# Two pairs of the MLP's first product in step, factors formed on VectorE, and x loaded by ScalarE

## The chip, the cores and the metric

One core of a Trainium2 chip runs the whole kernel. The metric is device time in microseconds, of the one core that is used.

## What is computed

One block of a transformer in float32, for x of 1024 tokens by 1024 features: a norm, a projection to queries, keys, values and gates, two kinds of attention (one with compressed, selected and windowed keys, one with a sliding window and a sink), and then what matters here:

```
y = sigmoid(gate_a) * (o_a @ w_up_nsa) + sigmoid(gate_b) * (o_b @ w_up_swa)
h = x + rms_norm(y @ w_out, norm_mix_post)
u = rms_norm(h, norm_mlp_pre)
f = square(relu(u @ w_mlp_in)) @ w_mlp_out        # 1024 -> 4096 -> 1024
out = h + rms_norm(f, norm_mlp_post)
```

## The kernel before, in words

The kernel is written in a tile language: the program states operations on named tiles and pools of buffers, and a scheduler puts them into one queue for each engine. It keeps to the order of the program as a priority, estimates times, and issues what is ready by that estimate, so the order on an engine can differ from that of the text. A pool has a number of buffers for each tag; a new tile of the tag waits until the tile that had its buffer has been read for the last time. Pools that are opened later lie on the memory of pools that were closed, and wait for their tiles in the same way.

**Float32 by three matmuls.** TensorE (PE) reads a reduced format. Each operand is therefore split into a high part (a copy by ScalarE into that format) and a low part (the difference of source and high part): `split`, L84 to L91. A product is high x high, high x low and low x high (`mm3`, L122 to L125; `prod`, L927 to L932). `load_w` (L95 to L116) loads a weight into a raw buffer, makes the high part on ScalarE (L107) and the low part in two pieces: columns of the first `cut` eighths on VectorE, the rest on GpSimd (L115, here 640 and 384 of 1024 columns). With `l_eng` given, one engine makes the whole low part (L105).

**Output projection.** `out_proj` (L806 to L830) is called four times, for two blocks of 128 tokens each; each call loads w_out again in eight pieces of 512 KB, issued by SP, with two raw buffers. The blocks of x that are added later (`load_x`, L834) are loaded by SP too: blocks 0, 1, 4 and 5 ahead of the first projection call, the others as buffers come free. `norm_a` adds x and writes h to memory, `norm_b` makes u, and `norm_t` (L855) transposes a block of u and forms factors of it.

**MLP, first product.** u @ w_mlp_in uses Winograd's form of Strassen's product: seven half-size products instead of eight, with factors that are sums of the quarters. The token half 0 gives the quarters 1 and 2 (bh0, bl0), made in `norm_t` of blocks 0 to 3, which also keep a float32 copy (braw). From `norm_t` of blocks 4 to 7, with its two transposed halves pts[0] and pts[1], come the factors 5, 3, 6, 4 and 7 for the right side:

```
t1 = pts[0] - braw_lo        # factor 5, low part by VectorE
b22 = pts[1]                 # factor 3, low part by GpSimd
t2 = b22 - t1                # factor 6, low part by VectorE
t4 = t2 - braw_hi            # factor 4, formed by GpSimd, low part by GpSimd
t3 = b22 - pts[0]            # factor 7, low part by GpSimd
```

All of this is done for the blocks 4 to 7 in `norm_t` (L870 to L877), with a small pool of four buffers. Products 1 and 2 need only the token half 0: `head` (L936 to L949) does them for a pair of column blocks of w_mlp_in. The heads of the first four pairs are issued ahead, beside the norms and transposes of blocks 5 to 7 (L953 to L961). `mlp1` (L973 to L1033) then goes through 16 pairs, one after the other: it loads two raw weights, has GpSimd form four sums of them (L992 to L995), splits five left operands (L998 to L1000), and does products 5, 3, 6, 4 and 7 of 12 matmuls each, with sums of their results (p5, c12, c21, c22) and, by GpSimd, four further sums q. Results go to memory for the second product. From pair 4 on, `mlp1` does its own head first: 84 matmuls a pair.

**What sets the order.** SP issues nearly all transfers, in one queue; where an issue waits for its buffer, those behind it wait too. VectorE, ScalarE and GpSimd run their queues in order. PSUM has six banks for results (tag ps) and two for transposes (tag pt); the four heads ahead hold four of the six.

Of the kernel before, what the change touches and what calls it, by code (L numbers as in the profile page):

```python
# [15 lines left out]
P = 128  # L16
# [36 lines left out]
def tile_hybrid_block(ctx: ExitStack, tc: tile.TileContext, x, norm_mix_pre, norm_mix_post, norm_mlp_pre,  # L53
# [39 lines left out]
    nw = [0]  # L93

    def load_w(parts, shape, wpool=None, hb=2, l_eng=None, rpool=None, rb=2, cut=5, tag="w"):  # L95
# [10 lines left out]
        else:  # L106
            nc.scalar.activation(h, raw, AF.Copy)  # L107
# [631 lines left out]
    with ExitStack() as s:  # L739
# [45 lines left out]
        wp2 = s_w2.enter_context(pool("wq"))  # L785
        s_e = s.enter_context(ExitStack())
# [10 lines left out]
        braw = ep.tile([P, NB, 512], F32, name="braw")  # L797
# [8 lines left out]
        def out_proj(c, ts_, nhs):  # L806
            pss = {(t, nh): ps_any() for t in ts_ for nh in nhs}
            n = 1024 // (512 * len(nhs))
            for k2 in range(NB // n):
                wh, wl = load_w([(None, wor[:, n * k2:n * k2 + n, 512 * nhs[0]:512 * nhs[-1] + 512])],  # L810
                                [n, 512 * len(nhs)], *((wp2, 2) if not started else (we, WEB)), cut=CUT[c], rpool=wp2)
# [22 lines left out]
        def load_x(b):  # L834
            hbs[b] = hb_e[b] if b in hb_e else (we if b < 4 else ea).tile([P, D], F32, name="hb", tag="hb", bufs=2)
            nc.sync.dma_start(hbs[b], x[b * P:(b + 1) * P, :])
# [18 lines left out]
        def norm_t(b):  # L855
# [4 lines left out]
            for k0 in range(0, NB, 4):  # L860
# [3 lines left out]
                if b < 4:  # L864
                    split(bh0[:, k0:k0 + 4, bs], bl0[:, k0:k0 + 4, bs], pt)
                    nc.scalar.activation(braw[:, k0:k0 + 4, bs], pt, AF.Copy)
# [3 lines left out]
            b22, t1, t3, t2, t4 = (e2.tile([P, 4, P], F32, name="bt", tag="bt", bufs=4) for _ in range(5))  # L870
            nc.scalar.activation(b22, pts[1], AF.Copy)
            nc.vector.tensor_tensor(t1, pts[0], braw[:, 0:4, bs], op=ALU.subtract)
            nc.vector.tensor_tensor(t3, b22, pts[0], op=ALU.subtract)
            nc.vector.tensor_tensor(t2, b22, t1, op=ALU.subtract)
            nc.gpsimd.tensor_tensor(t4, t2, braw[:, 4:8, bs], op=ALU.subtract)
            for i, (op_, src) in enumerate(((5, t1), (3, b22), (6, t2), (4, t4), (7, t3))):
                split(bh[op_][:, :, bs], bl[op_][:, :, bs], src, l_eng="pool" if i in (1, 3, 4) else "dve")  # L877

        load_x(0)
        load_x(1)  # L880
        load_x(4)
        load_x(5)
        out_proj(0, (0, 1), (0, 1))
# [6 lines left out]
        out_proj(0, (2, 3), (0, 1))  # L890
# [12 lines left out]
        e2 = s_e.enter_context(pool("e2"))  # L903
# [3 lines left out]
        for i in (5, 3, 6, 4, 7):  # L907
            bh[i] = u1.tile([P, 4, 512], F32R, name=f"bh{i}")
            bl[i] = u1.tile([P, 4, 512], F32R, name=f"bl{i}")
        bh[1], bl[1], bh[2], bl[2] = bh0[:, 0:4], bl0[:, 0:4], bh0[:, 4:8], bl0[:, 4:8]  # L910
# [42 lines left out]
        for p in range(NPRE):  # L953
            head(p, fp0, load_wcols(w_mlp_in, 2 * p * P, P, wp2, rpool=wp2))
# [4 lines left out]
            if p == 1:  # L959
                norm_t(6)  # L960
                norm_t(7)  # L961
        s_e.close()
# [4 lines left out]
        fp = s_m1.enter_context(pool("f"))  # L967
# [5 lines left out]
        def mlp1(p):  # L973
# [8 lines left out]
            if p in pre:  # L982
                xb, c11, _ = pre[p]
                s1 = fp.tile([P, 512], F32, name="p5", tag="p5", bufs=2)
# [50 lines left out]
        for p in range(NPAIR):  # L1035
            mlp1(p)
# [191 lines left out]
```

## Time and profile before

| what | value |
|---|---|
| median of three runs | 1590.59 us (1589.45 to 1592.19) |
| the profiled execution | 1591.69 us |
| its span, first to last instruction | 1589.9 us |
| mean granted clock of TensorE | 0.98 |
| PE busy (matmuls) | 1483.0 us, 93% of the span |
| VectorE (DVE) busy | 1068.0 us, 67% |
| ScalarE (ACT) busy | 749.0 us, 47% |
| GpSimd (POOL) busy | 488.8 us, 31% |
| memory traffic | 133 GB/s over the span |

The profile is that of one execution; its sums are held against its own time. Times inside it count from the start of the span. The output projection runs from about 794 to 918 us, the heads and transposes to 954, the pairs of `mlp1` to 1271, and then comes the second product. Where a line of the profile ends in a bracket, it gives the idle time of the engine before the instruction and what ended it. PE is TensorE, PEld its weight loads, SPq the queue of SyncE.

### The profile page before, as it was taken

What the parts mean: (1) busy time and instruction counts of PE and PEld (TensorE: products, weight loads), DVE (VectorE), ACT (ScalarE), POOL (GpSimd) and SP (SyncE); (2) the same over time, 40 slices, a digit from 0 to 9 for tenths busy, and PEclk for the clock granted to TensorE, in tenths of its full rate; (3) what the DMA queues carried; (4) which work ended last, traced back from release to release, by engine and by line L of the source; (5) the groups of instructions that cost most, each with busy time, mean ns of one, the idle gap of its engine ahead of it and who ended that gap; (6) DMA issues with size and microseconds to landing.
All of it is one profiled execution on the core that took longest, in us unless ns stands there. A gap on an engine that the chain in (4) does not pass through costs nothing. (4 is left out here: it accounts for less than half of the span.)

```text
span 1589.9 us, 20194 instructions
## 1 busy us (share of the span) xinstructions
PE 1483.0 (93%) x6920; PEld 1210.6 (76%) x6920; DVE 1068.0 (67%) x2070; ACT 749.0 (47%) x1453; POOL 488.8 (31%) x390
## 2 busy tenths in 40 slices
PE   6998999999999999999978885999999999999997
PEld 5897888778777787788756664787888778888886
DVE  5554774698865988836527686576766467495775
ACT  5343774566644776554236553332332324334443
POOL 3000351122311322331035457566666410000302
PEclk9999999999999999999989997999999999999999
DMA  7733124111132111164256652445443588353451
GB/s 210 248 98 81 37 57 146 45 39 34 31 97 61 37 34 38 34 235 151 69 206 213 210 156 67 140 156 164 155 147 128 205 314 323 98 185 112 153 186 53
DMA packets 162039, 204.80 MB, mean 129 GB/s; under 512 B 15120, under 2 KB 105264, under 8 KB 161936
## 3 DMA queue, kind: packets, MB, share of 16 engines
q1 hardware_dynamic: 154800, 182.78, 36.5%
q0 software_dynamic: 6992, 20.48, 3.6%
q8 instruction: 54, 0.88, 0.2%
q14 instruction: 49, 0.40, 0.1%
q10 hardware_dynamic: 144, 0.26, 0.0%
HBM read 153.02 MB, written 58.32 MB: 133 GB/s over the span
## 5 line engine op out<-in xcount | busy, mean ns | idle before, releaser
L123 PE MATMUL mm<-uh,wh 128*128 128x512 f32 x464 | 200.9, 433 | 4.6 <-DVE qb L447 3.2
L509 POOL TENSOR_TENSOR e<-e,w 128x256 f32<-128x256 f32 (+7 forms) x128 | 111.8, 900 | 284.2 <-DVE w L647 148.2
L124 PE MATMUL mm<-ul,wh 128*128 128x512 f32 x464 | 184.3, 397 | 0.0
L125 PE MATMUL mm<-uh,wl 128*128 128x512 f32 x464 | 184.2, 397 | 0.0
L87 ACT ACTIVATE th<-pt 128x512 fp32r<-128x512 f32 (+1 forms) x178 | 105.3, 593 | 94.7 <-PE pt L519 84.3
L501 ACT ACTIVATE e<-e,nm 128x256 f32<-128x256 f32 (+7 forms) x192 | 124.4, 649 | 36.1 <-DVE nm L495 35.5
L91 DVE TENSOR_TENSOR tl<-pt,th 128x512 fp32r<-128x512 f32 x162 | 110.1, 683 | 33.3 <-ACT th L87 32.1
L115 POOL TENSOR_TENSOR wl<-wraw,wh 128x384 fp32r<-128x384 f32 (+2 forms) x46 | 70.7, 1540 | 200.1 <-ACT wh L107 196.1
L87 ACT ACTIVATE fh<-fraw 128x1024 fp32r<-128x1024 f32 x56 | 59.6, 1063 | 148.0 <-PE xs L1121 70.2
L930 PE MATMUL ps<-bh,ws_h 128*128 128x512 f32 x256 | 102.9, 404 | 21.0 <-ACT ws_h L87 16.2
L91 DVE TENSOR_TENSOR fl<-fraw,fh 128x1024 fp32r<-128x1024 f32 x56 | 69.6, 1243 | 75.6 <-ACT fh L87 74.9
L519 PE MATMUL pt<-ident,e 128*128 128x128 f32 x648 | 104.4, 275 | 1.9 <-DVE e L512 0.9
L1144 POOL TENSOR_TENSOR cc<-cc,gB 128x512 f32<-128x512 f32 x14 | 24.3, 1762 | 262.4 <-ACT sq L1143 260.6
L125 PEld LDWEIGHTS mm<-uh,wl 128*128 128x128 f32 x464 | 87.6, 189 | 20.7
L1121 PE MATMUL xs<-vl,fh 128*128 128x512 f32 x256 | 99.7, 390 | 3.6 <-DVE vl L91 3.6
L931 PE MATMUL ps<-bl,ws_h 128*128 128x512 f32 x256 | 102.6, 401 | 0.0
L123 PEld LDWEIGHTS mm<-uh,wh 128*128 128x128 f32 x464 | 88.5, 191 | 18.1 <-issue 3.3
L932 PE MATMUL ps<-bh,ws_l 128*128 128x512 f32 x256 | 101.7, 401 | 0.2 <-DVE ws_l L91 0.2
L1121 PE MATMUL xs<-vh,fl 128*128 128x512 f32 x256 | 99.6, 389 | 0.0
L1121 PE MATMUL xs<-vh,fh 128*128 128x512 f32 x256 | 99.4, 389 | 0.0
L519 PEld LDWEIGHTS pt<-ident,e 128*128 128x128 f32 x648 | 81.4, 141 | 22.7 <-issue 2.3
L124 PEld LDWEIGHTS mm<-ul,wh 128*128 128x128 f32 x464 | 88.7, 191 | 12.0
(273 smaller groups left out, 3947.8 us busy)
## 6 DMA issues: line engine op xcount, KB each, us to landing
fraw<-f_d SPq DMA_DIRECT2D x48, 512.0 KB, 3.6
wraw<-in_w_mlp_in_dram SPq DMA_DIRECT2D x36, 512.0 KB, 4.2
wraw<-in_w_out_dram SPq DMA_DIRECT2D x32, 512.0 KB, 3.6
f_d<-q SPq DMA_DIRECT2D x64, 256.0 KB, 2.3
b<-in_w_mlp_out_dram SPq DMA_DIRECT2D x32, 512.0 KB, 10.8
wraw<-in_w_in_dram SPq DMA_DIRECT2D x27, 512.0 KB, 4.6
f_d<-c SPq DMA_DIRECT2D x48, 256.0 KB, 2.3
gate_d<-gst SPq DMA_DIRECT2D x32, 256.0 KB, 2.1
```

What stands on the lines that cost most here:

```text
L87: nc.scalar.activation(h, src, AF.Copy)
L91: eng.tensor_tensor(l, src, h.bitcast(F32), op=ALU.subtract)
L123: nc.tensor.matmul(ps, ah, bh, start=first, stop=False)
L124: nc.tensor.matmul(ps, ah, bl, start=False, stop=False)
L125: nc.tensor.matmul(ps, al, bh, start=False, stop=last)
L501: nc.scalar.activation(e[:, :n], e[:, :n], AF.Exp, scale=-1.0, bias=nm[:, r:r + 1], accum_out=sm[:, r:r + 1])
L509: nc.gpsimd.tensor_tensor(res[r][:, :n], res[r][:, :n], w[:, r:r + 1].to_broadcast([P, n]), op=ALU.mult)
L519: tr = nc.tensor.transpose(pt[:rows, r, :], es[r][:, off:off + rows], ident)
L930: nc.tensor.matmul(ps, ah[:, k, :], bh[i][:, k, :], start=n[0], stop=False, skip_group_check=True)
L931: nc.tensor.matmul(ps, ah[:, k, :], bl[i][:, k, :], start=False, stop=False, skip_group_check=True)
L932: nc.tensor.matmul(ps, al[:, k, :], bh[i][:, k, :], start=False, stop=n[1], skip_group_check=True)
L1121: nc.tensor.matmul(bank[t], l_[:, j, ts], r_[:, j, :], start=a_, stop=z_, skip_group_check=True)
```

## The change

- The factors 3, 6, 4 and 7 are no longer formed in `norm_t`. It forms factor 5 only and keeps both transposed halves in float32 (b12, b22, in the buffers that factor 7 takes later). A new function `factor(i, b)` forms one factor of one block, wholly by VectorE with the high part by ScalarE.
- The first two pairs of `mlp1` run in step, product by product: 5, 5, 3, 3, 6, 6, 4, 4, 7, 7. Factor 3 is formed ahead of them, factor 6 after the two products 5, factor 4 after the products 3, factor 7 after the products 6. `mlp1` becomes a generator; it splits each left operand just ahead of its product instead of all five together. From pair 2 on the pairs go one after the other as before.
- The low parts of the weights of the projection's second half (`c` = 1, eight loads in each of two calls) and of the four heads are made by VectorE alone.
- The x blocks 0 and 1 are issued by ScalarE behind the high part of weight 4 in the first projection call, the blocks 4 and 5 behind weight 3 in the second.
- Buffers: a new pool cq of eight 2 KB buffers holds the raw quarters (braw), and after them the results c and q; the pools of left operands and of p5 are cut differently; x blocks 0 to 3 have a pool of their own, which also holds t1.

```diff
+    last_act = [None]
@@ load_w
-            nc.scalar.activation(h, raw, AF.Copy)
+            last_act[0] = nc.scalar.activation(h, raw, AF.Copy)
@@
+        cq = s_w2.enter_context(pool("cq"))
+        braw = {(b, h): cq.tile([P, 4, P], F32, name="braw", tag="cq", bufs=8) for b in range(4) for h in range(2)}
@@
-        braw = ep.tile([P, NB, 512], F32, name="braw")
+        eh = s_e.enter_context(pool("etmph"))
+        hb_e.update({b: eh.tile([P, D], F32, name="hb", tag="hb", bufs=2) for b in (0, 1)})
@@
-        def out_proj(c, ts_, nhs):
+        def out_proj(c, ts_, nhs, xs_=(), at=0):
...
-                                [n, 512 * len(nhs)], *((wp2, 2) if not started else (we, WEB)), cut=CUT[c], rpool=wp2)
+                                [n, 512 * len(nhs)], *((wp2, 2) if not started else (we, WEB)), cut=CUT[c], rpool=wp2, l_eng="dve" if c else None)
+                if k2 == at:
+                    with tc.issue_after(last_act[0].ins):
+                        for b in xs_:
+                            load_x(b, nc.scalar)
@@ norm_t
-                    nc.scalar.activation(braw[:, k0:k0 + 4, bs], pt, AF.Copy)
+                    nc.scalar.activation(braw[b, k0 // 4], pt, AF.Copy)
...
-            b22, t1, t3, t2, t4 = (e2.tile([P, 4, P], F32, name="bt", tag="bt", bufs=4) for _ in range(5))
-            nc.scalar.activation(b22, pts[1], AF.Copy)
-            nc.vector.tensor_tensor(t1, pts[0], braw[:, 0:4, bs], op=ALU.subtract)
-            nc.vector.tensor_tensor(t3, b22, pts[0], op=ALU.subtract)
-            nc.vector.tensor_tensor(t2, b22, t1, op=ALU.subtract)
-            nc.gpsimd.tensor_tensor(t4, t2, braw[:, 4:8, bs], op=ALU.subtract)
-            for i, (op_, src) in enumerate(((5, t1), (3, b22), (6, t2), (4, t4), (7, t3))):
-                split(bh[op_][:, :, bs], bl[op_][:, :, bs], src, l_eng="pool" if i in (1, 3, 4) else "dve")
-
-        load_x(0)
-        load_x(1)
-        load_x(4)
-        load_x(5)
-        out_proj(0, (0, 1), (0, 1))
+            t1 = eh.tile([P, 4, P], F32, name="t1", tag="hb", bufs=2)
+            nc.vector.tensor_tensor(t1, pts[0], braw[b % 4, 0], op=ALU.subtract)
+            nc.scalar.activation(b12[:, :, bs], pts[0], AF.Copy)
+            nc.scalar.activation(b22[:, :, bs], pts[1], AF.Copy)
+            split(bh[5][:, :, bs], bl[5][:, :, bs], t1)
+
+        def factor(i, b):
+            hs = slice(b * P, (b + 1) * P)
+            lo_, hi_ = braw[b, 0], braw[b, 1]
+            if i == 3:
+                src = b22[:, :, hs]
+            elif i == 6:
+                nc.vector.tensor_tensor(b22[:, :, hs], b22[:, :, hs], b12[:, :, hs], op=ALU.subtract)
+                nc.vector.tensor_tensor(lo_, b22[:, :, hs], lo_, op=ALU.add)
+                src = lo_
+            elif i == 4:
+                nc.vector.tensor_tensor(hi_, lo_, hi_, op=ALU.subtract)
+                src = hi_
+                nc.scalar.activation(lo_, b22[:, :, hs], AF.Copy)
+            else:
+                if b == 0:
+                    bh[7], bl[7] = u7("bh7", F32R)
+                src = lo_
+            split(bh[i][:, :, hs], bl[i][:, :, hs], src)
+
+        out_proj(0, (0, 1), (0, 1), (0, 1), 4)
...
-        out_proj(0, (2, 3), (0, 1))
+        out_proj(0, (2, 3), (0, 1), (4, 5), 3)
@@ heads
-            head(p, fp0, load_wcols(w_mlp_in, 2 * p * P, P, wp2, rpool=wp2))
+            head(p, fp0, load_wcols(w_mlp_in, 2 * p * P, P, wp2, rpool=wp2, l_eng="dve"))
...
+        for b in range(4):
+            factor(3, b)
         s_e.close()
@@ mlp1
+            sm = w1a.tile([P, 4, P], F32, name="ws", tag="ws", bufs=3)
+            nc.gpsimd.tensor_tensor(sm, a21, a22, op=ALU.add)
...
-            sums = [w1a.tile([P, 4, P], F32, name="ws", tag="ws", bufs=3) for _ in range(4)]
-            for o, i0, i1, op_ in ((0, a21, a22, ALU.add), (1, sums[0], a11, ALU.subtract),
-                                   (3, a12, sums[1], ALU.subtract), (2, a11, a21, ALU.subtract)):
-                nc.gpsimd.tensor_tensor(sums[o], i0, i1, op=op_)
-            ops = {5: sums[0], 3: sums[3], 6: sums[1], 4: a22, 7: sums[2]}
-            hl = {}
-            for i, src in ops.items():
-                hl[i] = ab(w1a, "s1_", 1) if i == 5 else ab(w1, "ws_", 5)
-                split(*hl[i], src)
+            def left(i, src):
+                hl = ab(w1a, "s1_", 2) if i == 5 else ab(w1, "ws_", 4)
+                split(*hl, src)
+                return hl
...
+            prod(xb, *left(5, sm), 5, False, False)
+            p5 = f5.tile([P, 512], F32, name="p5", tag="p5", bufs=2) if not early else s1
             nc.vector.tensor_tensor(p5, xb, s1, op=ALU.subtract)
+            yield
+
+            for o, i0, i1 in ((sm, sm, a11), (a12, a12, sm), (a21, a11, a21)):
+                nc.gpsimd.tensor_tensor(o, i0, i1, op=ALU.subtract)
             yb = ps_any()
-            prod(yb, *hl[3], 3, True, True)
-            c12 = ft("c", 4)
+            prod(yb, *left(3, a12), 3, True, True)
+            c12 = ft("c")
             nc.scalar.activation(c12, yb, AF.Copy)
+            yield
...
-        for p in range(NPAIR):
-            mlp1(p)
+        two = [mlp1(0), mlp1(1)]
+        for i in (6, 4, 7, 0, 0):
+            for g in two:
+                next(g)
+            for b in range(4 if i else 0):
+                factor(i, b)
+        for p in range(2, NPAIR):
+            for _ in mlp1(p):
+                pass
```

## Rows read from the trace of the kernel before

**Rows 1.** Windows by stage: from:to, us, then busy (instructions) of each engine, clock, DMA.

```profile
794.00:806.00 12.00, 0.17 (x1) 0.17 (x2) 2.09 (x4) 1.69 (x2) 0.15 (x1) 0.68 0.93 329
860.00:918.00 58.00, 50.55 (x217) 37.17 (x216) 37.57 (x72) 31.74 (x57) 28.09 (x21) 1.00 0.59 197
918.00:936.00 18.00, 17.74 (x81) 14.01 (x80) 16.75 (x28) 12.64 (x26) 12.54 (x9) 1.00 0.45 128
936.00:954.00 18.00, 10.54 (x40) 7.71 (x40) 16.16 (x24) 6.80 (x14) 6.41 (x6) 0.81 0.59 191
954.00:970.00 16.00, 0.23 (x3) 0.00 (x0) 10.94 (x9) 5.68 (x11) 14.63 (x12) 0.54 0.12 35
970.00:1000.00 30.00, 26.93 (x103) 20.84 (x104) 17.52 (x20) 11.16 (x19) 17.05 (x12) 0.90 0.28 80
1100.00:1200.00 100.00, 100.00 (x433) 80.81 (x432) 66.97 (x80) 30.69 (x48) 60.71 (x41) 1.00 0.45 145
```

The engines in these rows are PE, PEld, DVE, ACT and POOL in this order; then come the granted clock, the DMA share and GB/s.

**Rows 2.** TensorE's waits, 790 to 1062 us: waiter, releaser, us, times, longest.

```profile
PE ps L123 <- ACT wh L107: 16.6, 6, 12.0
PE ps L930 <- ACT ws_h L87: 16.2, 1, 16.2
PE ps L930 <- ACT c L1021: 3.6, 2, 2.4
```

**Rows 3.** Timeline of SP, 792 to 800 us: start, duration, line, operation.

```profile
792.91 0.33 SPq L82 DMA_DIRECT2D gpost<-in_norm_mix_post_dram  x1
793.59 0.33 SPq L82 DMA_DIRECT2D gpre<-in_norm_mlp_pre_dram  x1
793.97 0.90 SPq L836 DMA_DIRECT2D hb<-in_x_dram  x2
794.91 2.13 SPq L99 DMA_DIRECT2D wraw<-in_w_out_dram  x2
797.15 1.19 SPq L836 DMA_DIRECT2D hb<-in_x_dram  x2
```

**Rows 4.** Timeline of ScalarE in the first projection call.

```profile
804.72 1.06 ACT L107 ACTIVATE wh<-wraw 128x1024 fp32r<-128x1024 f32 x1 [8.82 <-DMA wraw<-in_w_out_dram]
...
820.89 1.06 ACT L107 ACTIVATE wh<-wraw 128x1024 fp32r<-128x1024 f32 x1 [2.12 <-DMA wraw<-in_w_out_dram]
```

**Rows 5.** Timeline of TensorE: the longest wait in the heads.

```profile
943.69 0.80 PE L932 MATMUL ps<-bh,wl 128*128 128x512 f32 x1 [4.91 <-DVE wl L115]
```

**Rows 6.** Timelines of VectorE and GpSimd, 937 to 989 us.

```profile
937.97 4.93 DVE L91 TENSOR_TENSOR bl<-bt,bh 128x512 fp32r<-128x512 f32 x1
...
954.57 1.75 DVE L91 TENSOR_TENSOR bl<-bt,bh 128x512 fp32r<-128x512 f32 x1
...
988.12 0.68 DVE L91 TENSOR_TENSOR ws_l<-ws,ws_h 128x512 fp32r<-128x512 f32 x1
988.72 0.69 DVE L1023 SCALAR_TENSOR_TENSOR c<-c 128x512 f32<-128x512 f32 x1
...
939.87 2.47 POOL L91 TENSOR_TENSOR bl<-bt,bh 128x512 fp32r<-128x512 f32 x2
```

**Rows 7.** DMA issues, 780 to 930 us: KB each, median us to landing.

```profile
wraw<-in_w_out_dram SPq DMA_DIRECT2D x32, 512.0 KB, 3.6
hb<-in_x_dram SPq DMA_DIRECT2D x8, 512.0 KB, 6.6
```

**Rows 8.** Tile wraw: ns least, median, most; first and last start.

```profile
L115 POOL TENSOR_TENSOR wl<-wraw,wh x46: 280/1657/1826, 122.0 to 937.7; 128x384 fp32r<-128x384 f32 x44, 128x96 fp32r<-128x96 f32 x1, 128x48 fp32r<-128x48 f32 x1
L91 DVE TENSOR_TENSOR wl<-wraw,wh x33: 1210/1225/2307, 35.3 to 1215.4; 128x1024 fp32r<-128x1024 f32 x33
```

**Rows 9.** Tile bl: GpSimd's low parts of factors.

```profile
L91 POOL TENSOR_TENSOR bl<-bt,bh x12: 1251/1289/1928, 924.2 to 970.0; 128x512 fp32r<-128x512 f32 x12
```

**Rows 10.** Timeline of GpSimd: the first two sums of weights.

```profile
952.83 1.27 POOL L995 TENSOR_TENSOR ws<-wraw 128x512 f32<-128x512 f32 x1 [10.49 <-DMA wraw<-in_w_mlp_in_dram]
...
955.74 1.71 POOL L995 TENSOR_TENSOR ws<-ws,wraw 128x512 f32<-128x512 f32 x1
```

More of the change, by code (lines that the diff above doesn't have):

```diff
@@ L832, in tile_hybrid_block, with load_x @@
         ss2s = {}
-        def load_x(b):
-            hbs[b] = hb_e[b] if b in hb_e else (we if b < 4 else ea).tile([P, D], F32, name="hb", tag="hb", bufs=2)
-            nc.sync.dma_start(hbs[b], x[b * P:(b + 1) * P, :])
+        def load_x(b, eng=None):
+            hbs[b] = hb_e[b] if b in hb_e else (eh if b < 4 else ea).tile([P, D], F32, name="hb", tag="hb", bufs=2)
+            (eng or nc.sync).dma_start(hbs[b], x[b * P:(b + 1) * P, :])
         def norm_a(b):
@@ L902, in tile_hybrid_block @@
         s_y.close()
-        e2 = s_e.enter_context(pool("e2"))
         s_u2r = s.enter_context(ExitStack())
@@ L906, in tile_hybrid_block, with u7 @@
         bh, bl = {}, {}
-        for i in (5, 3, 6, 4, 7):
+        for i in (5, 3, 6, 4):
             bh[i] = u1.tile([P, 4, 512], F32R, name=f"bh{i}")
             bl[i] = u1.tile([P, 4, 512], F32R, name=f"bl{i}")
+        def u7(name, dt):
+            return [u1.tile([P, 4, 512], dt, name=name + t, tag="u7" + t) for t in "hl"]
+        b12, b22 = u7("b_", F32)
         bh[1], bl[1], bh[2], bl[2] = bh0[:, 0:4], bl0[:, 0:4], bh0[:, 4:8], bl0[:, 4:8]
@@ L966, in tile_hybrid_block @@
         w1 = s_m1.enter_context(pool("w1"))
-        fp = s_m1.enter_context(pool("f"))
+        f5 = s_m1.enter_context(pool("f5"))
         def ab(p_, tag, bufs):
@@ L981, in mlp1 @@
             a11, a12, a21, a22 = raw[0][:, 0:4], raw[0][:, 4:8], raw[1][:, 0:4], raw[1][:, 4:8]
-            if p in pre:
+            sm = w1a.tile([P, 4, P], F32, name="ws", tag="ws", bufs=3)
+            nc.gpsimd.tensor_tensor(sm, a21, a22, op=ALU.add)
+            early = p in pre
+            if early:
                 xb, c11, _ = pre[p]
-                s1 = fp.tile([P, 512], F32, name="p5", tag="p5", bufs=2)
+                s1 = f5.tile([P, 512], F32, name="p5", tag="p5", bufs=2)
                 nc.scalar.activation(s1, xb, AF.Copy)
@@ L1002, in ft @@
-            def ft(tag, bufs):
-                return fp.tile([P, 512], F32, name=tag, tag=tag, bufs=bufs)
-            prod(xb, *hl[5], 5, False, False)
-            p5 = ft("p5", 2)
+            def left(i, src):
+                hl = ab(w1a, "s1_", 2) if i == 5 else ab(w1, "ws_", 4)
+                split(*hl, src)
+                return hl
+            def ft(tag):
+                return cq.tile([P, 512], F32, name=tag, tag="cq", bufs=8)
+            prod(xb, *left(5, sm), 5, False, False)
@@ L1011, in mlp1 @@
             nc.scalar.activation(c12, yb, AF.Copy)
-            prod(xb, *hl[6], 6, False, False)
+            yield
+            prod(xb, *left(6, sm), 6, False, False)
             nc.vector.tensor_tensor(c12, xb, c12, op=ALU.add)
+            yield
             yb = ps_any()
-            prod(yb, *hl[4], 4, True, True)
+            prod(yb, *left(4, a22), 4, True, True)
             nc.vector.tensor_tensor(p5, yb, p5, op=ALU.add)
-            prod(xb, *hl[7], 7, False, True)
-            c21 = ft("c", 4)
+            yield
@@ L1019, in mlp1 @@
+            prod(xb, *left(7, a21), 7, False, True)
+            c21 = ft("c")
             nc.vector.tensor_tensor(c21, xb, p5, op=ALU.subtract)
-            c22 = ft("c", 4)
+            c22 = ft("c")
             nc.scalar.activation(c22, xb, AF.Relu)
@@ L1024, in mlp1 @@
             nc.vector.tensor_tensor(c22, c22, c22, op=ALU.mult)
-            q = [ft("q", 4) for _ in range(4)]
+            q = [ft("q") for _ in range(4)]
             eng = nc.gpsimd if p < NPAIR - 1 else nc.vector
@@ L1033, in mlp1 @@
                 nc.sync.dma_start(f_d[i][p], t)
-        for p in range(NPAIR):
-            mlp1(p)
+            yield
+        two = [mlp1(0), mlp1(1)]
[7 more added lines that the diff above has]
+                pass
         s_m1.close()
```

## Prediction

> **What bounds the kernel now.** I read the windows by stage first, then TensorE's waits, then the timelines around the longest waits. The page of the profile has PE at 93%, and in the long middle of the MLP's first matrix product it is at its limit: 433 matmuls in 100 us, 0.231 us each, at full clock [rows 1]. Nothing in that stretch can be gained by the change, since it leaves the number of matmuls alone. What can be gained lies where PE stands, between 794 and 1060 us. [Rows 2] list those waits: 16.6 us on the high part of the output projection's weights (12.0 in one piece), 16.2 us in one piece on the high part of the MLP's left operands, 3.6 us on a Relu. A further one, 4.91 us on the low part of a weight, stands in [rows 5]. The reader should see in [rows 1] that the stretch of 954 to 970 us has 0.23 us of PE in it and 14.63 of POOL, and that the ones beside it run at a mean clock of 0.81 and 0.90.
>
> **The 12 us at the start of the output projection.** SP issues six transfers of 512 KB: the two gain vectors, two blocks of x, the first two weights, then two more blocks of x [rows 3]. DMA moves 329 GB/s at a share of 0.93 [rows 1], so it is the bound there. The first weight is issued with four transfers ahead of it and ScalarE gets it at 804.72, after 8.82 us of idling on that DMA [rows 4]. The change takes x off this front. Two blocks of x were ahead: 1.05 MB at 329 GB/s is 3.2 us, the least that can go. The most: the first weight, issued when x was (793.97), takes the usual 3.6 us of such a load [rows 7] and ScalarE starts at 797.6, 7.1 us earlier. The gain vectors lie in between: a new 16 KB pool shifts them onto memory that is released earlier, so they may leave a few us sooner. I take 5.
>
> The x blocks come back later, four of them beside the weights of the first two projection calls, issued by ScalarE. There a weight is ready with ScalarE idle 2.12 us before it [rows 4], so there is slack, but little. If x loads cost the weights nothing, 0; if each pair of blocks holds the weights up for its full 3.2 us less 1.1 us of slack (half of the 2.12), 4.2 in all. I take 2, because in [rows 7] x loads take 6.6 us against 3.6 of a weight: they share, they don't queue in full. The issue itself is about 0.4 us each on SP [rows 3]; four on ScalarE are 1.6 us beside matmuls, behind the split of a weight and ahead of the next one, which waits for its own DMA meanwhile. Their buffers are new, so the issues wait for nothing. Net: **-3** (bounds -7 and +1). Two further x loads stay on SP and are not moved.
>
> The Trainium skill, "DMA: Bandwidth & Descriptors", section "Issuing engines are not separate DMA queues", says that transfers issued by ScalarE, SyncE or GpSimd run on the same 16 DMA engines and interleave, so that another issuer saves issue time alone. By that rule the later x loads cost nearer 4 than 0, and this part would come out at -1.
>
> **Low parts of the weights by VectorE alone** (second half of the projection, and the four heads). Before, VectorE made 640 of 1024 columns and GpSimd 384; GpSimd's part took 1.657 us and ended last, VectorE's whole would take 1.225 [rows 8]. A raw buffer is therefore free 0.43 us earlier, 16 times, and the window 860 to 918 has 7.45 us without PE [rows 1]. VectorE is busy 65% there, so it has room, though its queue also carries the norms. I take **-1.5** (bounds -4 and +1, the latter if a norm's step now stands behind each of 16 splits that are 0.4 us longer).
>
> **The heads, 936 to 954.** PE is busy 10.54 of 18 us; the longest wait is 4.91 us on a low part of a weight [rows 1, 5]. [Rows 6] show why: VectorE's split of a factor, 0.68 us when alone, is stretched to 4.93 us, and ends only when two splits on GpSimd have ended (939.87+2.47 = 942.34). The weight's low part stands behind it on VectorE. With the change GpSimd's 12 splits of factors [rows 9] and its 4 subtractions are gone, so this wait goes and its slow clock goes with it: 7.5 us without PE, and of (1-0.81) x 18 = 3.4 us at the lower clock the half that I put on matmuls, 1.7 [rows 1]. Next late are the transposes of the last two blocks, which need their norm; I leave 2.2. **-7** (bounds -9 and -2).
>
> **The factors, 954 to 976.** Before, PE waits 16.2 us [rows 2] because all five factors of all four blocks, and the sums of the weights, come ahead of the first product; then its clock is down: (1-0.90) x 30 = 3 us [rows 1]. Together 19. With the change only factor 5 is needed to start (formed in the transposes' step: one subtraction and one split for each block), and products 5, 3, 6, 4, 7 of two pairs, 24 matmuls or 5.6 us a step, cover the next factor.
>
> Does the cover suffice? After factor 5, VectorE issues for four blocks: factor 3, 4 instructions; 6, 12; 4, 8; 7, 4. That is 28, and before product 4 can start 24 of them, 8 low parts of left operands, two differences p5 and two sums c12: 36 at 0.60 us apart uncontended [rows 6], 21.6 us. Products 5, 3 and 6 of two pairs give 16.8 us, and I suppose factor 3 (2.4 us) to be done in the heads. So VectorE is late by 21.6-2.4-16.8 = 2.4 us, if alone. GpSimd still makes 4 sums of weights for each pair, eight, some 1.3 to 1.7 us each [rows 10], and a VectorE instruction beside one takes 1.75 instead of 0.68 [rows 6]. Four of the eight overlapping costs 4 x 1.1 = 4.4 us, all eight 8.8. I take 4.4, since the sums come in two bursts and the first ones run while VectorE still waits for product 5. Late by **7**; bounds 2 and 11. ScalarE's share (high parts and copies) runs beside it: it is busy 11.16 of 30 us in 970 to 1000 [rows 1].
>
> Two waits are added. The low part of product 3's left operand stands behind factor 6 on VectorE if that is issued in program order: part of the 7. And the c12 copies on ScalarE wait for a slot in the pool of the raw blocks, which factor 4 frees; behind them stand the high parts of left operands 6 and 4. Product 4 waits for factor 4 anyway, so I cost that at nothing; without that cover it is one factor step, 4.8 us. GpSimd's first sum waited 10.49 us for its DMA [rows 10], which was queued on SP behind the late weight; this goes with the head's wait. So **-12** (19-7; bounds -17 and -8).
>
> The Trainium skill, "SBUF — State Buffer", section "Who interferes with whom", says that a VectorE instruction with two inputs in SBUF and a GpSimd instruction that reads SBUF exclude one another for the whole instruction. The 4.93 us row agrees with it. It speaks against VectorE being free here: by that rule all eight sums block it, and this part would be -8.
>
> **The pairs behind, and the rest.** Behind the factors PE waits 3.6 us on Relus [rows 2]; a different set of buffers may move this either way, I take **0** (bounds -3 and +4: pair 2's raw weights can only be loaded once the lockstep has read those of pairs 0 and 1, one load of some 4 us). From 1060 on, nothing: PE is full.
>
> **Sum:** -3 -1.5 -7 -12 = -23.5 us. The profiled execution took 1591.69 us with a span of 1589.9 (1.8 lie outside); 1591.7-23.5 = 1568.2. The median of the runs shown, 1590.59, is 1.1 below the profiled one, so **1567**. All bounds at their good ends give -40, at their bad ends -4.
>
> **Rivals.**
> - *The cover is complete.* VectorE runs ahead, the stall is gone altogether and the front gains its 7: -7 -2 -8 -18 -1 = -36, 1555. For it: of five instructions a block VectorE keeps two in the heads. Against: it is busy 16.75 of 18 us in 918 to 936, and that has to take factor 3 as well [rows 1]. Chance 0.2.
> - *VectorE becomes the bound of the lockstep.* All eight sums collide and every step waits, with the clock down again (3 us): -3 -1 -4 -5 +1 = -12, 1579. For it: [rows 6]. Chance 0.2.
> - *Slower than before.* The lock between GpSimd and VectorE, in the lockstep alone. If GpSimd is never idle there (sums, then the q's of pair 0), each of the 28 factor instructions and the 10 left splits costs 1.75 instead of 0.60, 38 x 1.15 = 43.7 us more, in place of the 4.4 in the sum: 1567+43.7-4.4 = 1606. It is level with before from some 20 further collisions on (23.5/1.15). Against: eight sums of 1.3 us are 10 us, in 28 us of products. With milder mixtures above 1594, chance 0.07.
> - *No difference.* The gain in the factors is paid back by the x loads and pair 2: 0.05. That the reordering isn't what the scheduler emits (it chooses the order of issue by its own estimates) is in these last two.
>
> **How the numbers follow.** The forecast has 0.48, and its own range is 1558 to 1577. With the rivals on the fast side and the VectorE-bound one the range is **1551 to 1584**. A measurement tells 0.2%, 3.2 us, from no change. Faster: 0.48+0.2+0.2 = 0.88; the same 0.05, slower 0.07.
>
> **What would show it.** Right: PE's first projection matmul within 9 us of the last gated one instead of 12; no POOL splits of factors; no single PE wait over 7 us between 936 and 985; the second pair's product 7 ended by about 980; windows past 1100 unchanged at 433 matmuls per 100 us. The step on the cover is wrong if PE waits before products 3 or 6 sum to over 11 us or to nothing; the step on x is wrong if weights of the first two calls are late by over 4 us. The whole is wrong if waits of a kind not listed here (the pool's slots, SP's queue) exceed 10 us.

## The result, and the profile after

The changed kernel takes **1577.85 us** (median of four runs, 1575.44 to 1580.5) where the kernel before takes 1591.39 on the same chip: a ratio of 0.9915, 95% interval 0.9891 to 0.9939. That is 13.5 us less; 23.5 were forecast, and 1567 with a range of 1551 to 1584. The direction was right and the time lies in the range, but more than two fifths of the gain are missing. The profiled execution took 1580.5 us with a span of 1578.7, 11.2 less than the span before; the account below is of these two executions. This one is the slowest of the four. Run a8_factors_first below turned out to be the same kernel in its queues, and was profiled at 1575.47 us; where the two traces differ, the text says so.

Three points of TensorE's timeline divide the span: the first matmul of the projection, the first of product 5 of pair 0, and the first of the second product.

| stretch | before, us | after, us | difference | forecast |
|---|---|---|---|---|
| start to the projection's first matmul | 805.83 | 799.74 | -6.1 | -5 |
| projection, to the first head's matmul | 112.16 | 112.94 | +0.8 | +0.5 (x +2, low parts -1.5) |
| heads and factors, to product 5 | 52.49 | 34.45 | -18.0 | -23 (heads -7, the wait of 16.2) |
| product 5 to the second product | 300.22 | 310.61 | +10.4 | +4 (7 late, 3 of clock won back, pairs behind 0) |
| the rest | 319.2 | 321.0 | +1.8 | 0 |

The forecast gives -12 for the factors as one number; the table puts its terms where they belong in time. By them product 5 should have started some 5 us earlier still, and the products behind it were to lose 4. They lose 10.4: 6.8 us in waits (11.7 instead of 4.9) and 3.6 in matmuls that ran slower (298.9 us busy instead of 295.3, for the same matmuls). In the repeat a8 this stretch loses 7.5, 6.6 in waits and 0.9 in slower matmuls. The windows of the changed kernel, with the columns of [rows 1], show where:

```profile
794.00:806.00 12.00, 7.40 (x26) 5.63 (x25) 3.84 (x5) 3.64 (x4) 3.19 (x2) 0.86 0.64 220
860.00:918.00 58.00, 54.39 (x236) 42.61 (x235) 44.04 (x84) 35.34 (x65) 2.16 (x4) 0.97 0.64 210
918.00:936.00 18.00, 18.00 (x87) 15.02 (x86) 17.69 (x36) 12.28 (x22) 1.06 (x2) 1.00 0.55 169
936.00:954.00 18.00, 5.49 (x19) 3.82 (x18) 17.61 (x22) 10.64 (x21) 8.24 (x5) 0.60 0.31 87
954.00:970.00 16.00, 14.38 (x48) 10.56 (x47) 12.21 (x15) 5.76 (x11) 5.06 (x3) 0.81 0.24 66
970.00:1000.00 30.00, 29.83 (x128) 23.44 (x127) 24.29 (x24) 9.48 (x17) 21.57 (x14) 1.00 0.41 126
1000.00:1060.00 60.00, 54.68 (x225) 42.49 (x223) 45.37 (x44) 15.73 (x27) 40.42 (x26) 0.97 0.47 152
1100.00:1200.00 100.00, 100.00 (x433) 80.84 (x432) 67.25 (x78) 29.91 (x47) 58.82 (x42) 1.00 0.45 146
```

Against [rows 1]: 860 to 918 has 54.39 us of PE instead of 50.55, and the hole of 954 to 970 is filled (14.38 instead of 0.23). But 936 to 954 has fallen from 10.54 to 5.49, at a clock of 0.60, with VectorE busy 17.61 of 18 us. The MLP's long middle is unchanged at 433 matmuls per 100 us.

TensorE's waits of the changed kernel, 936 to 1062 us (waiter, releaser, us, times, longest), take the place of the 16.2 and 3.6 us of [rows 2] and the 4.91 of [rows 5]:

```profile
PE pt L872 <- DVE o L862: 4.6, 1, 4.6
PE ps L957 <- ACT s_h L87: 4.1, 1, 4.1
PE ps L959 <- DVE s_l L91: 3.8, 1, 3.8
PE ps L957 <- DVE c L1046: 2.4, 1, 2.4
PE ps L959 <- DVE ws_l L91: 1.8, 3, 1.2
PE ps L957 <- ACT c L1056: 1.2, 1, 1.2
PE ps L957 <- DVE p L1035: 1.0, 1, 1.0
PE ps L957 <- ACT ws_h L87: 0.7, 2, 0.5
```

They sum to 19.6 us; taken the same way from 930 us on, before had 27.8. The first is new: the transposes of block 7 (tile pt) wait for its norm (o, L862). The tiles s_h and s_l are the high and low part of product 5's left operand, ws_h and ws_l those of the later products; p is the sum p5. VectorE's timeline of the changed kernel says what kept the norm:

```profile
930.94 1.28 DVE L91 TENSOR_TENSOR bl<-braw,bh 128x512 fp32r<-128x512 f32 x2
932.14 0.68 DVE L894 TENSOR_TENSOR braw<-b_l,braw 128x512 f32<-128x512 f32 x1
...
934.67 0.67 DVE L897 TENSOR_TENSOR braw<-braw 128x512 f32<-128x512 f32 x1
935.26 0.68 DVE L91 TENSOR_TENSOR bl<-braw,bh 128x512 fp32r<-128x512 f32 x1
...
939.66 1.27 DVE L862 SCALAR_TENSOR_TENSOR o<-hb,rs_o,gpre 128x1024 f32<-128x1024 f32 x1
...
945.07 3.10 DVE L91 TENSOR_TENSOR bl<-braw,bh 128x512 fp32r<-128x512 f32 x2 [0.26 <-ACT bh L87]
948.10 1.75 DVE L91 TENSOR_TENSOR bl<-b_l,bh 128x512 fp32r<-128x512 f32 x1
949.88 1.63 DVE L893 TENSOR_TENSOR b_l<-b_l,b_h 128x512 f32<-128x512 f32 x1
951.44 0.68 DVE L91 TENSOR_TENSOR s_l<-ws,s_h 128x512 fp32r<-128x512 f32 x1
...
952.64 1.77 DVE L91 TENSOR_TENSOR s_l<-ws,s_h 128x512 fp32r<-128x512 f32 x1
...
954.94 3.47 DVE L91 TENSOR_TENSOR bl<-braw,bh 128x512 fp32r<-128x512 f32 x2
958.34 2.98 DVE L91 TENSOR_TENSOR bh7l<-braw,bh7h 128x512 fp32r<-128x512 f32 x3
```

L894 forms factor 6 and L897 factor 4, of the first blocks. The text has them behind products 5 and 3 of both pairs, but the scheduler issues them ahead of the last block's norm, because their sources are ready. Between 920 and 940 there are 13 instructions of factors 3, 6 and 4, 0.60 us apart, 7.8 us. So all factors are formed by 962.5, when TensorE has done little more than product 5 of both pairs: the products cover next to nothing. From 944.24 GpSimd's sums run beside them, and from 945 to 958 seven of VectorE's instructions take 1.55 to 1.77 us instead of 0.68 (a row of x2 holds two). GpSimd's timeline of the same stretch:

```profile
944.24 1.70 POOL L1012 TENSOR_TENSOR ws<-wraw 128x512 f32<-128x512 f32 x1 [14.20 <-DMA wraw<-in_w_mlp_in_dram]
946.02 1.60 POOL L1039 TENSOR_TENSOR wraw<-wraw,wraw 128x512 f32<-128x512 f32 x1
947.59 1.71 POOL L1012 TENSOR_TENSOR ws<-wraw 128x512 f32<-128x512 f32 x1
```

The low part s_l, which product 5 needs, stands behind these stretched splits and starts at 951.44: the 3.8 us wait. The 4.1 us ahead of it, on s_h, aren't the lock's: with the sums on VectorE (a4 and b1 below) the same 4.1 us remain, ended by ScalarE's copy for p5. GpSimd's first sum, too, stands until 944.24 on a DMA, that of its raw weight.

### The profile page after: what moved, and what is told of

The parts are those of the page before. It is cut to its first block, busy times and chain, and to the rows that moved or that the text cites. A ratio compares the mean times of both kernels' runs of the same rounds, so it can differ in the third digit from the quotient of the medians.

```text
span 1578.7 us, 20103 instructions
## 1 busy us (share of the span) xinstructions
PE 1487.3 (94%) x6920; PEld 1214.2 (77%) x6920; DVE 1088.4 (69%) x2086; ACT 751.2 (48%) x1461; POOL 439.8 (28%) x354
## 5 line engine op out<-in xcount | busy, mean ns | idle before, releaser
L87 ACT ACTIVATE fh<-fraw 128x1024 fp32r<-128x1024 f32 x56 | 59.4, 1062 | 145.3 <-PE xs L1165 78.3
L87 ACT ACTIVATE wh<-wraw 128x1024 fp32r<-128x1024 f32 x69 | 73.0, 1058 | 111.1 <-PE mm L125 36.7
L91 DVE TENSOR_TENSOR wl<-wraw,wh 128x1024 fp32r<-128x1024 f32 x53 | 69.0, 1301 | 45.9 <-ACT wh L87 45.5
L116 POOL TENSOR_TENSOR wl<-wraw,wh 128x384 fp32r<-128x384 f32 (+2 forms) x26 | 38.7, 1493 | 161.7 <-ACT wh L108 161.7
L91 POOL TENSOR_TENSOR wl<-wraw,wh 128x1024 fp32r<-128x1024 f32 x16 | 38.6, 2410 | 159.5 <-ACT wh L87 159.5
## 6 DMA issues: line engine op xcount, KB each, us to landing
b<-in_w_mlp_out_dram SPq DMA_DIRECT2D x32, 512.0 KB, 10.8
```

The costliest lines, as they stand in the source:

```text
L87: nc.scalar.activation(h, src, AF.Copy)
L91: eng.tensor_tensor(l, src, h.bitcast(F32), op=ALU.subtract)
```

## The experiments

Theory at the outset: VectorE and GpSimd hold each other up (the lock), and the scheduler's order makes the cover useless. Rivals: the x loads cost the gain; the order alone does; VectorE has simply too much work. Each kernel is the changed one with the edit named. All ratios are to the kernel before on the same chip, with 95% intervals.

| run | median, us | ratio |
|---|---|---|
| changed kernel | 1577.85 | 0.9915 (0.9891 to 0.9939) |
| a1_x_front | 1577.78 | 0.9901 (0.9886 to 0.9916) |
| a2_x_sp | 1575.99 | 0.9889 (0.9874 to 0.9904) |
| a3_order | 1576.72 | 0.9895 (0.9877 to 0.9914) |
| a4_sums_dve | 1572.00 | 0.9865 (0.9850 to 0.9880) |
| a5_pool_w | 1582.44 | 0.9928 (0.9912 to 0.9944) |
| a7_serial | 1574.14 | 0.9877 (0.9861 to 0.9893) |
| a8_factors_first | 1575.37 | 0.9901 (0.9881 to 0.9920) |
| a9_factors_pool | 1583.46 | 0.9933 (0.9917 to 0.9949) |
| b1_sums_q_dve | 1567.01 | 0.9840 (0.9820 to 0.9860) |
| c1_serial_dve | 1567.34 | 0.9842 (0.9827 to 0.9858) |
| c2_strict_dve | 1569.88 | 0.9858 (0.9837 to 0.9879) |
| c4_dve_sq | 1569.46 | 0.9855 (0.9837 to 0.9873) |

**The x loads: a1_x_front, a2_x_sp.**

```
a1: +for b in (0, 1, 4, 5): load_x(b)          # ahead of the first call, by SP
    -out_proj(0, (0, 1), (0, 1), (0, 1), 4)    +out_proj(0, (0, 1), (0, 1))
a2: -load_x(b, nc.scalar)                      +load_x(b)
```

> The changed kernel with the four x loads back where they were: issued by SP ahead of the first projection call. Theory 'x costs its place': the first projection matmul comes 5 to 7 us later again (after an idle time of 11 to 12 us instead of 4.6), and the first two calls lose their waits beside the x loads (about 4 us of PE time between 806 and 860). Net 1 to 3 us slower than the changed kernel, some 1580. Rival 'the x loads are hidden where the change puts them': no gain in the two calls, so 6 to 7 us slower, some 1584.

> The changed kernel with the x loads at the same places in the program, but issued by SP instead of ScalarE. Theory 'the 16 DMA engines are shared, the issuer is not the point': the time stays within 2 us of the changed kernel's 1578, and the waits beside the x loads stay. Rival 'a second issuer lets the x loads overtake the weights': with SP alone the x loads queue ahead of the next weights in one line, which then are later: 3 to 6 us slower.

Undoing the part loses nothing: 1577.8, less than theory (1580) and rival (1584) gave. In its trace TensorE waits 7.38 us for its first matmul of the projection, not 11 to 12; the changed kernel waits 4.60 and the one before 12.04. Counted from the start of the span, the matmul comes 2.3 us later than in the changed kernel, and 3.8 earlier than in the one before:

```profile
802.01 2.07 PE L124 MATMUL ps<-wh,yh 128*128 128x512 f32 x4 [7.38 <-ACT wh L108]
```

The projection itself then takes 110.16 us instead of 112.94. Its first two calls, in which the x loads lie, take 54.5 us here, 57.7 in the changed kernel and 57.1 to 58.8 in the eleven other runs that keep x there. By these traces the part is worth -2.8 at the front and +3.1 behind it, nothing net. The other 4.7 us of the wait (12.04 less 7.38) aren't the x loads': SP's first issue, gpost, leaves at 791.04 (792.91 in [rows 3]), and ScalarE waits 4.15 us for the first weight instead of 8.82 [rows 4]. What made gpost leave earlier, a pool that moved as the prediction supposed, was not tried by itself. With SP as the issuer the time stays within 2 us: who issues is not the point.

**Low parts of the weights: a5_pool_w.**

```
-... rpool=wp2, l_eng="dve" if c else None)     +... rpool=wp2)
-load_wcols(..., wp2, rpool=wp2, l_eng="dve")   +load_wcols(..., wp2, rpool=wp2)
```

> Edit: the low parts of the weights of the second half of the projection and of the four heads are shared with GpSimd again (5 parts of 8 on VectorE, 3 on GpSimd), as before the change; all else is the changed kernel. Theory (VectorE is the bound from 918 to 963 us, and GpSimd's tensor work holds VectorE up for as long as it lasts, so GpSimd's share is no relief): the projection's second half gives back the 3.4 us that it had gained, nothing comes back in the heads, 1581. Rival (VectorE is simply overfull, and each of 12 weights takes 0.46 us off it): VectorE is 5 us earlier at the factors, 1575.

1582.4, near the theory's 1581 and not the rival's 1575. The window shows PE back from 54.39 to 52.26 and POOL from 2.16 to 28.69 us:

```profile
860.00:918.00 58.00, 52.26 (x229) 39.91 (x229) 38.14 (x74) 32.41 (x56) 28.69 (x21) 1.00 0.64 204
```

The intervals of this run and the changed kernel overlap. By the medians the part is worth 4.6 us (7.1 against the repeat), by the ratios 2 to 4, by the window 2.1 (3.0 against the repeat's 55.26): its sign is likely, its size isn't pinned down. GpSimd's share is no relief for VectorE later: the time did not fall.

**Factors by VectorE alone: a9_factors_pool.**

```
-split(bh[i], bl[i], src)
+split(bh[i], bl[i], src, l_eng="dve" if i == 6 else "pool")
```

> Edit: the low parts of factors 3, 4 and 7 (12 instructions) go to GpSimd, as before the change; order and lockstep stay. Theory (the two engines exclude one another): VectorE loses 12 x 0.6 = 7.2 us of work but GpSimd adds 12 x 1.3 to 1.7 us, some 18 us in which VectorE's two-input instructions stand: slower by about 8 us, 1586. Rival (VectorE has too much work and GpSimd has time): faster by up to 7 us, 1571.

1583.5: the theory's sign and, by the medians, most of its size (5.6 of 8; 3 to 5 by the ratios, whose intervals overlap, but all five executions are slower than the ten of the changed kernel and its repeat). VectorE is as full as in the changed kernel with three instructions fewer in 936 to 954 (17.95 us for 19, there 17.61 for 22), and GpSimd works 13.76 us beside it instead of 8.24:

```profile
936.00:954.00 18.00, 7.82 (x29) 5.39 (x28) 17.95 (x19) 11.09 (x21) 13.76 (x9) 0.63 0.31 87
954.00:970.00 16.00, 10.97 (x35) 7.52 (x34) 7.97 (x9) 5.71 (x10) 12.20 (x9) 0.82 0.17 46
```

**The written order: a8_factors_first.**

```
+for i in (6, 4, 7):
+    for b in range(4): factor(i, b)
 for i in (6, 4, 7, 0, 0):
     for g in two: next(g)
-    for b in range(4 if i else 0): factor(i, b)
```

> Edit: in the program's text all of factors 6, 4 and 7 stand ahead of the lockstep instead of between its products. The order of instructions that comes out of the scheduler is the changed kernel's on VectorE, ScalarE, GpSimd and TensorE through the whole of these two pairs. Theory (the scheduler decides, the written order does not): the changed kernel's time, 1578, within 3 us. Rival (the prediction's, that the written order is what covers the factors): 16.8 us of cover lost, 1590 or more.

1575.4, and the waits of 930 to 1062 us sum to 19.7 where the changed kernel has 19.6. Where the factors are written decides nothing: the queues come out the same. This also repeats the changed kernel: the two medians are 2.5 us apart, so a difference of that size between two runs means nothing here.

**The lockstep: a7_serial.**

```
 for i in (6, 4, 7, 0, 0):
-    for g in two: next(g)
+    next(two[0])
     for b in range(4 if i else 0): factor(i, b)
+for _ in two[1]: pass
```

> Edit: the lockstep alone is undone: the factors stand between the products of the first pair, and the second pair follows as a whole. Theory (the scheduler emits all factors ahead of the products that were to cover them, wherever they are written, so the lockstep covers next to nothing): within 3 us of the changed kernel, 1578. Rival (the prediction's: 5.6 us of products of two pairs cover each factor; with one pair only 2.8 do): three factors lose 2.8 us each, 1586.

1574.1: without the lockstep it is no slower, and if anything 1 to 4 us faster by the medians. The rival falls. The gain lies behind the factors, in a window where the changed kernel has 54.68 us of PE and its repeat 55.19:

```profile
1000.00:1060.00 60.00, 57.75 (x246) 45.53 (x245) 47.26 (x47) 17.84 (x31) 42.92 (x27) 1.00 0.47 157
```

In lockstep, pairs 0 and 1 end together. Their eight q and the sums of pairs 2 to 4 then make nearly one run on GpSimd, from 977.46 to 1011, and VectorE's instructions take up to 1.79 us in it. One after the other, that work is spread: it begins at 969.48 and has gaps of 2.92 and 4.64 us.

**The order on VectorE and ScalarE: a3_order.**

```
+with tc.issue_after(<both halves of block 7's split of factor 5>):
     for b in range(4): factor(3, b)
```

> The changed kernel with the factors 3, 6, 4 and 7 held, in issue order only, behind factor 5 of the last block on VectorE and ScalarE. Theory 'factors too early': in the changed kernel 13 factor instructions (8 us of VectorE) stand ahead of the norm of block 7 and delay product 5; with the order fixed the transposes of block 7 come by 936 instead of 941, the first product starts 5 to 8 us earlier, and products 3 and 6 cover the factors, so 5 to 9 us faster than the changed kernel, some 1570. Rival 'VectorE is full anyway': the same work moves behind product 5 and is waited for there; within 2 us of 1578.

1576.7: the theory of the order falls, and the rival's time (within 2 us of 1578) comes out. The transposes of block 7 no longer wait. But VectorE, which the held factors had kept busy, now idles on s_h, which waits for GpSimd's sum; that low part stands ahead of block 7's factor, and the locked stretch comes right behind:

```profile
937.24 1.20 DVE L91 TENSOR_TENSOR s_l<-ws,s_h 128x512 fp32r<-128x512 f32 x1 [2.75 <-ACT s_h L87]
...
941.26 1.75 DVE L91 TENSOR_TENSOR s_l<-ws,s_h 128x512 fp32r<-128x512 f32 x1
942.94 1.75 DVE L91 TENSOR_TENSOR bl<-t,bh 128x512 fp32r<-128x512 f32 x1
```

**GpSimd's sums, then its q, on VectorE: a4_sums_dve, b1_sums_q_dve.**

```
+seng = nc.vector if p < 2 else nc.gpsimd       # a4: the four sums of pairs 0 and 1
-nc.gpsimd.tensor_tensor(sm, a21, a22, op=ALU.add)
+seng.tensor_tensor(sm, a21, a22, op=ALU.add)   # and the three subtractions
-eng = nc.gpsimd if p < NPAIR - 1 else nc.vector
+eng = nc.gpsimd if 1 < p < NPAIR - 1 else nc.vector   # b1, on top: their q
```

> The changed kernel with the eight sums of the weights of pairs 0 and 1 on VectorE instead of GpSimd, so that GpSimd has nothing to do between 940 and 975. Theory 'the lock': VectorE instructions take 0.68 us each instead of up to 1.77 from 945 to 960, which saves some 8 us of VectorE against 4.8 us of added work; product 5 is ready 2 to 4 us earlier; some 1575. Rival 'the sums come too late for another reason' (the raw weights' DMA, the order on VectorE): no gain, or up to 3 us slower by the added instructions.

> Edit: on top of the kernel with the weight sums of the first two pairs on VectorE (1572.0), the four combinations q of these two pairs go to VectorE too; GpSimd still makes sums and q of the later pairs. Theory (behind the factors the lead is given back because GpSimd's sums of pairs 2 and 3 and the q of pairs 0 and 1 run back to back and stretch VectorE's instructions from 0.68 to some 1.75 us): the PE waits of 1000 to 1060 us, some 4 us in all, go, 1568. Rival (the waits there come from raw weights that are loaded late): 1572, or above it by the 8 x 0.6 = 4.8 us that VectorE gets.

1572.0 and **1567.0**, where the theories have some 1575 and 1568. In a4 VectorE has eight more instructions, and the time falls by 5.9 us against the changed kernel's median (3.4 against the repeat). Product 5 does not start earlier, which the theory wanted too (34.7 us behind the first head, 34.5 in the changed kernel); what goes is the wait just behind its start. In a4's trace of VectorE the sums and the splits beside them take 0.68 us each:

```profile
945.60 0.68 DVE L1013 TENSOR_TENSOR ws<-wraw 128x512 f32<-128x512 f32 x1
946.21 1.28 DVE L91 TENSOR_TENSOR bl<-braw,bh 128x512 fp32r<-128x512 f32 x2
947.41 0.68 DVE L91 TENSOR_TENSOR bl<-b_l,bh 128x512 fp32r<-128x512 f32 x1
```

With the q there too, these are all of TensorE's waits from 936 to 1062 us, 13.0 instead of 19.6:

```profile
PE pt L872 <- DVE o L862: 4.9, 1, 4.9
PE ps L957 <- ACT p L1018: 4.1, 1, 4.1
PE ps L957 <- DVE c L1047: 2.0, 2, 1.5
PE ps L959 <- DVE ws_l L91: 2.0, 2, 1.5
```

The 3.8 us on s_l are gone. From a4 to b1 the waits of 1000 to 1060 us fall from 4.1 to 1.5. The intervals of these two overlap, so the 5.0 us between their medians are less sure than the 10.8 of both steps together (8.4 against the repeat). This version beats both kernels, and its interval lies clear of theirs.

**On top of it: c1_serial_dve, c2_strict_dve, c4_dve_sq.**

```
c1: b1 and a7
c2: b1, and   +with tc.issue_after(<left operands of product 5, pair 1>): factors 3 and 6
              +with tc.issue_after(<... of product 3>): factor 4;  (<... of 6>): factor 7
              +with tc.issue_after(<block 7's split of factor 5>): first sums
c4: b1, and in the four heads
    -nc.vector.scalar_tensor_tensor(c11, c11, 0.0, c11, op0=ALU.max, op1=ALU.mult)
    +nc.scalar.activation(c11, c11, AF.Relu)
    +nc.scalar.activation(c11, c11, AF.Square)
```

> Edit: sums and combinations of the first two pairs on VectorE (1567.0), and the lockstep undone (1574.1 by itself). Theory (the lockstep's harm is GpSimd's work of four pairs in one run behind it; with most of that off GpSimd it is already gone): 1566, within 3 us of 1567. Rival (the two gains are of different kinds and add up, 3.7 us more): 1563.

> Edit: sums and combinations of the first two pairs on VectorE, in lockstep, and the order that the change wanted now forced on the scheduler: the sums behind the last block's factor 5, factors 3 and 6 behind the left operands of product 5, factor 4 behind those of product 3, factor 7 behind those of product 6. Theory (VectorE's work sets the pace from 918 to 962 us, in whatever order): the first product starts some 5 us earlier, waits before the later products sum to 4 us more, 1566 (1563 to 1569). Rival (the cover is worth what the prediction said once the order is really emitted): 1559.

> Edit: on top of the kernel with sums and combinations of the first two pairs on VectorE (1567.0), the squared Relu of the four heads' products leaves VectorE: ScalarE does it in two instructions, Relu and Square. Theory (VectorE's work sets the pace from 918 to 962 us, so each instruction taken off it gives its 0.6 us): 4 x 0.6 = 2.4 us, 1564.6. Rival (it is the order and the chains through ScalarE, which gets 8 more instructions of 0.6 us): 1567 or up to 3 us above.

c1: 1567.3, the gains don't add, as the theory has it: with this work off GpSimd, the lockstep does no harm that can be seen. c2 has the order that the change wanted in its queues, and is no faster: 1569.9 (1565.3 to 1575.8). Product 5 starts at 936.37 instead of 945.04 (2.5 us of this lie ahead of the heads), but TensorE's timeline then has its waits inside the lockstep, and the last one behind it:

```profile
936.37 0.80 PE L959 MATMUL ps<-bh,s_h 128*128 128x512 f32 x1 [4.08 <-ACT s_h L87]
948.57 0.80 PE L961 MATMUL ps<-bh,ws_l 128*128 128x512 f32 x1 [2.81 <-DVE ws_l L91]
957.00 0.51 PE L960 MATMUL ps<-bl,ws_h 128*128 128x512 f32 x1 [1.72 <-DVE bl L91]
...
981.83 0.50 PE L961 MATMUL ps<-bh,ws_l 128*128 128x512 f32 x1 [3.11 <-DVE ws_l L91]
```

From 930 to 1062 us its waits sum to 13.1, b1's to 13.0: the order only moves them. VectorE ends the last factor at 964.2 here and at 959.5 in b1; it is full from 934 until then. So the cover's rival (1559) falls. The theory's way of counting is borne out here, though the median lies 0.9 us over its 1563 to 1569; c4 does not bear it out: VectorE is relieved of 2.4 us, product 5 starts 3.9 us earlier, and the time doesn't fall: 1569.5, inside the rival's 1567 to 1570. In c4 the start falls into a stretch of low clock (0.63; b1 has 0.72):

```profile
936.00:954.00 18.00, 13.21 (x41) 9.73 (x42) 17.30 (x29) 12.90 (x24) 0.00 (x0) 0.63 0.22 63
```

13.21 us of PE for 41 matmul and transpose records, where b1 does 38 in 10.90. From product 5 to the second product c4 takes 7.0 us longer than b1: 3.2 of waits and 3.7 of slower matmuls. What limits b1 further, VectorE's amount of work or the chain norm, transpose, split, p5 copy (4.9 + 4.1 us), stays open.

## Why the prediction was right or wrong

- **The front, -5:** right in size (-6.1; the wait itself fell by 7.4, from 12.04 to 4.60 us), and partly luck. "Two blocks of x were ahead: 1.05 MB at 329 GB/s is 3.2 us, the least that can go": a1 gives 2.8 for them. The larger part, 4.7, isn't theirs: gpost leaves 2.7 us earlier against the last gated operand, which the prediction had only as "may leave a few us sooner", and no run shows what moved it, or where the other 2.0 come from. (Two counts were wrong, and nothing hangs on them: [rows 3] have eight such transfers, not six, and four x loads stay on SP, not two.)
- **Later x loads, +2:** too small, some 3.1. Weights were late by 5.0 us in the first two calls, over the 4 that the prediction named as its sign of error, but 3.2 of them are there in a1 too. The Trainium skill, "DMA: Bandwidth & Descriptors", "Issuing engines are not separate DMA queues", says that transfers of all issuers share the DMA engines and interleave; the prediction took nearer 4 from it, and the 3.1 lie between. a2 agrees with it that the issuer isn't the point.
- **Low parts by VectorE, -1.5:** right in sign as far as the runs tell, some 2 to 7.
- **The heads, -7:** the wait of 4.91 us went, as the step said, since GpSimd makes no splits of factors any more; 918 to 936 now has 18.00 us of PE. "Next late are the transposes of the last two blocks, which need their norm; I leave 2.2" was the right next wait and too small: 4.6. That "its slow clock goes with it" did not hold: 936 to 954 has 0.60 instead of 0.81.
- **The factors, -12: the step that failed.** It is that "products 5, 3, 6, 4, 7 of two pairs, 24 matmuls or 5.6 us a step, cover the next factor". The scheduler formed factors 6 and 4 of the early blocks in the heads too, which delayed block 7's norm, and all factors by 962.5, when product 3 had just begun. So the products covered next to nothing, and TensorE's waits between them are some 1.7 us, not the 7 by which VectorE was to be late. In their place 4.1 and 3.8 us came at product 5 itself, where the prediction had no wait. The stated worry that the reordering isn't emitted had a share of 0.12, as a harm only. It is what happened, and it cost little by itself: a8, a3 and c2 show that neither the written nor the emitted order moves the time by more than 3 us, and by a7 the lockstep gave nothing that can be seen.
- **The end of the lockstep:** the second pair's product 7 ends at 986 (981.9 in the repeat), not by about 980 as the prediction wanted.
- **The lock, +4.4 for four of eight sums:** right mechanism, mis-sized, and misplaced. a4 measures 3.4 to 5.9 for the sums of two pairs, net of the eight sums that VectorE then makes itself (4.8 us at 0.60). The prediction put it between the products; it struck the splits ahead of s_l. The Trainium skill, "SBUF — State Buffer", "Who interferes with whom", has a VectorE instruction with two inputs in SBUF and a GpSimd instruction that reads SBUF exclude one another; from that the prediction let all eight sums collide and got -8 for the factors. VectorE's seven stretched instructions between 945 and 958, beside eight sums of 1.59 to 1.72 us each, side with it.
- **The pairs behind, 0:** mis-sized by a few us. The prediction looked at pair 2's late raw weights. The waits behind the lockstep are 5.3 us where the kernel before has 3.6, and b1 and a7 put part of them down to GpSimd's run of q and sums beside VectorE: moving the q took 5.0 us more off (b1 against a4, by the medians).
- **Sum.** Heads, factors and pairs: -7.6 instead of -19 (-9.6 by the repeat's trace); the rest of the span +1.8. The forecast's own range, 1558 to 1577, was missed by 0.9 us; the time lies in the stated one because that took in the rival at 1579. This rival, "VectorE becomes the bound of the lockstep", is the nearest, though its waits lie ahead of product 5's low part rather than at every step. Those at 1555 (cover complete) and 1606 (lock throughout) didn't come. How much of the 18.0 us ahead of product 5 is owed to fewer factors being needed there, and how much to GpSimd's splits being gone, no run separates; a9 puts the splits of three factors back and loses 5.6.

## What to carry to other kernels

Look at the queue that comes out, not at the text: a scheduler issues what is ready, and work that was to be hidden behind later work can land ahead of what is urgent. Moving work off GpSimd can pay where VectorE is full beside it, in the same stretch and in the one where GpSimd's leftovers gather; adding 16 instructions to the busy engine was worth 8 to 11 us here. Work can hide behind another engine's only if the engine that does it has slack: in the changed kernel VectorE was busy 35.3 of the 36 us from 918 to 954, and no order of its work that was tried gained anything.

## What the runs showed of the hardware

TensorE's clock can make a wait dearer than its length. In the changed kernel, after a wait of 2.39 us the next matmuls follow each other at 0.43 us instead of 0.23, until 1035.40, some 1.6 us on top:

```profile
1028.86 0.39 PE L957 MATMUL ps<-bh,ws_h 128*128 128x512 f32 x1
1031.65 0.62 PE L957 MATMUL ps<-bh7h,ws_h 128*128 128x512 f32 x1 [2.39 <-DVE c L1046]
1032.06 0.63 PE L958 MATMUL ps<-bh7l,ws_h 128*128 128x512 f32 x1
...
1035.40 0.39 PE L957 MATMUL ps<-bh7h,ws_h 128*128 128x512 f32 x1
```

Eight of them are at the lower level, 1.2 GHz; the granted clock is 0.66 over 1031 to 1036. But the same wait ahead of the same matmul leaves the clock at 1.00 in the repeat a8:

```profile
1027.77 0.51 PE L957 MATMUL ps<-bh7h,ws_h 128*128 128x512 f32 x1 [2.39 <-DVE c L1046]
1028.12 0.39 PE L958 MATMUL ps<-bh7l,ws_h 128*128 128x512 f32 x1
1028.35 0.39 PE L959 MATMUL ps<-bh7h,ws_l 128*128 128x512 f32 x1
```

So one trace can't give the price of such a wait, and it is part of why two executions of one kernel differ. From 942 to 954 us of the changed kernel the clock is 0.50 throughout, over two waits of about 4 us and the few matmuls between them; there the repeat has the same (0.50 from 940 to 952). An earlier start gains little while waits like these stand behind it; c4 fits that, but no run shows it by itself.

GpSimd suffers in the lock too: the same sum of 512 columns takes it some 1.3 us at the least (1.29 at 977.46) and 1.59 to 1.72 beside VectorE's splits. VectorE does it in 0.68 (a4).
